# A one-core diffusion block: the residual's scale inside the gated additions, its gated bias in the next MLP quarter

## Chip, cores and metric

The kernel runs on one core of a Trainium2 chip. The metric is the device time of one execution in microseconds; the kernel before is given by the median of three runs. The profile is of one further execution of the same program.

## What is computed

The reference is one step of a one-layer backbone for 640 tokens (128 of a context, 512 of a latent) of width 1024: a token mixer, then a squared-ReLU MLP, each with a residual and a layer norm. The change touches only the residual of the MLP:

```python
h2 = layer_norm(x) * (1.0 + mod[:, 4]) + mod[:, 3]
f = jnp.square(jax.nn.relu(h2 @ w_mlp1 + b_mlp1)) @ w_mlp2 + b_mlp2
x = layer_norm(DEEPNORM_ALPHA * x + mod[:, 5] * f, ln2_g, ln2_b)
```

With gate g = mod[:, 5], the sum in the last line is alpha * x + g * b_mlp2 + g * (hidden @ w_mlp2). The gate differs between context and latent tokens, so there are two rows of it.

## The kernel before, in words

**Tiles and stages.** The 640 tokens lie in five tiles of 128 tokens; `x1s` holds them as five fp32 tiles of 128 x 1024. fp32 products are made in TensorE's fp32r format from two parts: `wsplit` (L324 to L329) has SP load a weight tile of 128 x 1024 (`wr`, two buffers), ACT casts its high part (L321) and DVE subtracts to get the low part (L322); both parts go to one tile (`wh`, three buffers). Three matmuls (high by high, high by low, low by high: `PASS`) make one product, and only the last of them needs DVE's low part.

**The MLP.** The hidden width of 4096 is done in four quarters of 1024. A quarter first makes its hidden tiles `fx` (eight of 128 rows, two parts each), then multiplies them by its quarter of `w_mlp2` (L1061 to L1076): for either half `fh` of the 1024 output columns there are four weight tiles (index `kp`), each with two steps of k, five token tiles and three passes, so 30 matmuls of 512 columns a weight tile, 120 a half and 240 a quarter (L1073). Below, a weight tile of the first half is called kp0 to kp3 and one of the second half kp0' to kp3'. A half's sums lie in PSUM: two tiles of two banks (`ps`, token tiles 0 and 1, then 2 and 3) and one bank. There are three of the two-bank tiles, so the second tile of the second half takes the place of the first tile of the first half, and may be written only after that one has been read by `add_gated` (L849 to L852): DVE multiplies the sum in PSUM by the gate (L851), then adds it to the `x1s` tile (L852).

**The first quarter** makes its hidden tiles with plain matmuls (L913, L926), and does three things besides. `gates` (L773 to L787) builds the two gate tiles `g5`: DVE adds a bias row (L778), the row goes to DRAM (`grd`, L779), and two DMAs spread it over the 128 partitions (L783). `rhs_sums` (L946 to L974), a generator that advances one step after each `wsplit`, makes sums of `h2` for the later quarters, whose first products use a scheme with fewer multiplications (`mlp_pair`, L999); its DVE lines are L953 to L972 and, through `split`, L322. And `residual` (L1042 to L1046) runs once, after the second weight tile: for each token tile DVE makes tmp = b2 * g5 (L1045) and x = alpha * x + tmp (L1046). Its row b2 is loaded at L1056 by `brow_tile` (L764 to L767), which repeats one row of DRAM over the 128 partitions. The second and third quarters take their hidden tiles from `mlp_in8`; the fourth is written apart and not touched.

**What sets the order.** Engines run their instructions in program order, one queue each. That order is not the text's: a scheduler, which works with the priorities of the text and a model of durations, places each instruction when the kernel is built, and tiles wait for a free buffer of their pool. The MLP's fp32 work tiles come from one pool of nine (`x4`); five are the `x1s` tiles, b2 and the tmp tiles are others.

Of the kernel before, what the change touches and what calls it, by code (L numbers as in the profile page):

```python
# [14 lines left out]
ALU = mybir.AluOpType  # L15
AX = mybir.AxisListType

P = 128
D = 1024
# [9 lines left out]
ALPHA = 2.0 ** 0.25  # L29
# [9 lines left out]
def hybrid_kernel(ctx: ExitStack, tc: tile.TileContext, xin, cc, w_ada0, w_ada, w_in, w_glu, w_pa, w_pool, w_pb,  # L39
                  w_out, w_m1, w_m2, cols, rows, brow, lam, bpk, cpk, ddg, s0, cst, invc, out, nstate):  # L40
    nc = tc.nc
    V, S, T = nc.vector, nc.scalar, nc.tensor
# [24 lines left out]
    def sub_tile(tag, bufs, pool=None):  # L67
        return lambda shape, name: (pool or sub[0]).tile(shape, F32, tag=tag, bufs=bufs, name=nm(name))
# [3 lines left out]
    def bank2(name="ps"):  # L72
        return pp[0].tile([P, 2, 512], F32, tag="mm", name=nm(name))
# [231 lines left out]
    for t in range(NTT):  # L305
        x = mat4([P, D], "x")
# [447 lines left out]
    x4 = sub_tile("x4", 9)  # L754
# [9 lines left out]
    def brow_tile(src, tile_of, name="brow"):  # L764
        t = tile_of([P, D], name)
        dma(t, src.broadcast_to([P, D]))
        return t  # L767
# [37 lines left out]
    for m in range(KT):  # L805
        ps = gps[m] if m < 2 else mm(wsplit(w_glu[m]), vx)
# [16 lines left out]
    x1s = []  # L823
    for t in range(NTT):
        x = x4([P, D], "x1")
# [3 lines left out]
    for m in range(KT):  # L829
# [4 lines left out]
        ps = mm(wsplit(w_pa[m]), [gx[:, k] for k in range(KT)])  # L834
# [7 lines left out]
        if m < NTT:  # L842
            tmp = x4([P, D], "tmp")
# [2 lines left out]
    ada4.cols(row_tile(), 3, True)  # L846


    def add_gated(x, g, ps, c0, c1):  # L849

        V.tensor_tensor(ps, ps, g[:, c0:c1], op=ALU.mult)  # L851
        V.tensor_tensor(x[:, c0:c1], x[:, c0:c1], ps, op=ALU.add)  # L852

    def ln_mv():
        return keep.tile([P, 2], F32, tag="mv", bufs=4, name=nm("mv"))
# [23 lines left out]
    for t in range(NTT):  # L879
        st = 0 if t else 1  # L880
        x = x1s[t]
        ps = bank2()
# [12 lines left out]
        tmp = x4([P, D], "tmp")  # L895
        V.tensor_scalar(tmp, x, mv[:, 0:1], rs, op0=ALU.subtract, op1=ALU.mult)
        hf = x4([P, KT, P], "h2f")
        for h in range(2):
            pt = bank("pst")
# [3 lines left out]
            for i in range(4):  # L903
                k = 4 * h + i
                S.activation(hf[:, k, :], pt[:, i * P:(i + 1) * P], AF.Identity,
                             scale=modc[:, 3, k, st:st + 1], bias=modc[:, 2, k, st:st + 1])
# [39 lines left out]
    def rhs_sums():  # L946
        b11, b12, b21, b22 = [h2[:, :, 4 * i:4 * i + 4, j * HN:(j + 1) * HN] for i in range(2) for j in range(2)]
        t1, t2, t4 = [w10("t").rearrange("p a (k c) -> p a k c", k=4) for _ in range(3)]
        rq.update(b11=b11, b21=b21, b22=b22, t1=t1, t2=t2, t3=b12, t4=t4)

        def whole(b, k):
            f = x4([P, 2, HN], "bf")
            V.tensor_tensor(f, b[:, 0, k:k + 2].bitcast(F32), b[:, 1, k:k + 2].bitcast(F32), op=ALU.add)  # L953
            return f

        def put(t, k, f):
            split(f, t[:, 0, k:k + 2], t[:, 1, k:k + 2])

        for k in (0, 2):
            f12, f11 = whole(b12, k), whole(b11, k)  # L960
            V.tensor_tensor(f11, f12, f11, op=ALU.subtract)
            put(t1, k, f11)
            yield
            f22 = whole(b22, k)
            V.tensor_tensor(f12, f22, f12, op=ALU.subtract)
            put(b12, k, f12)
            yield
            V.tensor_tensor(f22, f22, f11, op=ALU.subtract)
            put(t2, k, f22)
            yield  # L970
            f21 = whole(b21, k)
            V.tensor_tensor(f21, f21, f22, op=ALU.subtract)  # L972
            put(t4, k, f21)
            yield  # L974
# [64 lines left out]
    def mlp_in8(m):  # L1039
        return [f for i in range(0, 8, 2) for f in mlp_pair(m + i)]  # L1040

    def residual():  # L1042
        for t in range(NTT):
            tmp = x4([P, D], "tmp")
            V.tensor_tensor(tmp, b2, g5[0 if t else 1], op=ALU.mult)  # L1045
            V.scalar_tensor_tensor(x1s[t], x1s[t], ALPHA, tmp, op0=ALU.mult, op1=ALU.add)  # L1046

    for qf in range(3):
        if qf == 0:
            ada5.load(2)  # L1050
            fx = mlp_first()
            for i, n in ((5, 3), (6, 3), (7, 2)):
                ada5.step(n)
                if i == 7:
                    g5 = gates(ada5, 1)
                    b2 = brow_tile(brow[3:4, :], x4)  # L1056
                fx.append(mlp_in(i))
        else:
            fx = mlp_in8(qf * 8)
        sums = rhs_sums() if qf == 0 else iter(())  # L1060
        for fh in range(2):  # L1061
            pa, pb, pc_ = bank2(), bank2(), bank("ps4")
            pt = [pa[:, 0], pa[:, 1], pb[:, 0], pb[:, 1], pc_]
            for kp in range(4):
                hl = wsplit(w_m2[fh, qf * 4 + kp])
                next(sums, None)
                if qf + fh == 0 and kp == 1:
                    residual()
                for kk in range(2):
                    k = 2 * kp + kk  # L1070
                    for t in range(NTT):
                        for i, (wh, xh) in enumerate(PASS):
                            T.matmul(pt[t], fx[k][:, xh, t * P:(t + 1) * P], hl[:, wh, kk * 512:(kk + 1) * 512],  # L1073
                                     start=(k == 0 and i == 0), stop=(k == 7 and i == 2))
            for t in range(NTT):
                add_gated(x1s[t], g5[0 if t else 1], pt[t], fh * 512, fh * 512 + 512)  # L1076

    fx = mlp_in8(24)
    lg2, lb2 = brow_tile(brow[4:5, :], x4), brow_tile(brow[5:6, :], x4)
# [1 line left out]
    for t in range(NTT):  # L1081
        last = t == NTT - 1
        if t == 0:
            ps2 = bank2()
            ps = [ps2[:, 0], ps2[:, 1]]
        else:
            ps = [bank("pse")] + ([bank2()[:, 0], bank2()[:, 0]] if last else [bank("pse")])

        parts = [(0, 0, 512), (1, 0, 256), (1, 256, 256)] if last else [(0, 0, 512), (1, 0, 512)]
        x = x1s[t]  # L1090
        for k, n in [(k, n) for k in range(8) for n in range(2)] if t == 0 else \
                [(k, n) for n in range(len(parts)) for k in range(8)]:
            fh, o, ln = parts[n]
# [102 lines left out]
```

## Time and profile before

| | us |
|---|---|
| median of three runs | 1059.72 |
| the three runs | 1059.72, 1054.45, 1062.24 |
| the profiled execution | 1057.73 |
| its span | 1056.0 |
| first quarter's 240 output matmuls, first start to the next block's | 672.10 to 733.71 |

The span is the time between the first and the last instruction of the profiled execution; its own time has 1.7 us around it. Times within the trace count from the span's start. A row of the timeline merges instructions of one line: start, length, engine, line, operation, what it writes and reads, count, and in brackets the idle time of the engine before it with what ended that.

### The profile page before, as it was taken

The numbers are of one execution on the slowest core, as the hardware profiler recorded it, in microseconds if no ns is written. First come the engines' busy times: TensorE is split into PE (matmuls) and PEld (weight loads), VectorE is DVE, ScalarE is ACT, GpSimd is POOL, SyncE is SP. The second block draws the span as 40 slices with busy tenths as digits, with TensorE's granted clock in tenths as the row PEclk, the third lists the DMA queues.
The fourth block names the chain that finished last, engine by engine and source line by source line (L and its number), as shares of the span: only waits on it lengthen the run. The fifth ranks groups of instructions, "written<-read, shape, count | busy, mean of one in ns | idle before, by whom it ended". The sixth has DMA issues, their size and how long they took to land.

```text
span 1056.0 us, 18416 instructions
## 1 busy us (share of the span) xinstructions
PE 991.3 (94%) x7464; PEld 894.4 (85%) x7464; DVE 691.6 (65%) x1203; ACT 403.0 (38%) x683; POOL 110.9 (11%) x164
## 2 busy tenths in 40 slices
PE   4998989998998899999999999989999999999997
PEld 2887878988897799998987898868998899889886
DVE  7698769998921334545847955498864586458686
ACT  5457454322212534422222544313661266116610
POOL 0243210310069000300000000000000000000000
PEclk9999899999999798999999999999999999999999
DMA  9566666855498587977752134513222222212421
GB/s 362 191 176 179 168 182 194 255 166 170 119 284 248 161 253 244 360 231 252 247 182 83 31 110 155 150 45 100 81 100 73 68 80 100 80 60 81 162 78 60
DMA packets 117373, 166.85 MB, mean 158 GB/s; under 512 B 48104, under 2 KB 80872, under 8 KB 117288
## 3 DMA queue, kind: packets, MB, share of 16 engines
q1 hardware_dynamic: 111912, 146.27, 43.9%
q0 software_dynamic: 5376, 19.40, 5.4%
q8 instruction: 59, 0.97, 0.4%
q14 instruction: 26, 0.21, 0.1%
HBM read 135.30 MB, written 30.34 MB: 157 GB/s over the span
## 4 chain that ended last, share of the span: by engine, by line
PE 61%; DVE 16%; DMA 10%; issue 6%; ACT 5%; SPq 2%; DVEq 0%; ACTq 0%; POOL 0%; POOLq 0%
PE ps L336 20%; PE ps L1073 13%; PE ps L1006 8%; PE psx L1006 6%; PE pse L1096 3%; PE ps L886 3%; DVE wh L322 2%; DMA cf<-in_cpk_dram 2%; DMA yd<-y 2%; DVE ta L501 1%; DVE zt L504 1%; PE psa L236 1%; PE psz L480 1%; DVE ta L503 1%; PE ps L1096 1%
## 5 line engine op out<-in xcount | busy, mean ns | idle before, releaser
L336 PE MATMUL ps<-hk,wh 128*128 128x320 f32 x1344 | 217.1, 318 | 10.0 <-DVE sq L542 5.1
L336 PEld LDWEIGHTS ps<-hk,wh 128*128 128x128 f32 x1344 | 202.0, 192 | 18.6 <-issue 6.0
L322 DVE TENSOR_TENSOR wh<-wr,wh 128x1024 fp32r<-128x1024 f32 (+1 forms) x113 | 128.5, 1138 | 101.8 <-ACT wh L321 100.7
L321 ACT CAST wh<-wr 128x1024 fp32r<-128x1024 f32 (+1 forms) x113 | 109.3, 967 | 164.7 <-PE ps L1073 87.6
L1073 PE MATMUL ps<-wh,fx 128*128 128x512 f32 x720 | 166.1, 392 | 5.2 <-DVE x L852 3.0
L1073 PEld LDWEIGHTS ps<-wh,fx 128*128 128x128 f32 x720 | 135.7, 189 | 34.2 <-DVE x L852 3.4
L336 PEld LDWEIGHTS ps<-gx,wh 128*128 128x128 f32 x384 | 56.4, 187 | 3.3 <-issue 2.9
L336 PE MATMUL ps<-gx,wh 128*128 128x320 f32 x384 | 58.7, 310 | 0.0
L336 PEld LDWEIGHTS ps<-vx,wh 128*128 128x128 f32 x384 | 56.4, 188 | 2.5 <-ACT sg L813 2.1
L336 PE MATMUL ps<-vx,wh 128*128 128x320 f32 x384 | 58.1, 311 | 0.0
L224 POOL DMA_DIRECT2D wa<-in_w_ada_dram x32 | 16.9, 534 | 300.8 <-PE psa L236 110.2
L1006 PE MATMUL psx<-h,wh 128*128 128x320 f32 x288 | 47.5, 308 | 0.0
L1006 PE MATMUL ps<-h,w 128*128 128x320 f32 x288 | 46.5, 307 | 0.0
L438 POOL TENSOR_TENSOR cf<-cf 128x64 f32<-128x64 f32 x32 | 24.8, 776 | 191.0 <-DMA cf<-in_cpk_dram 95.7
L1006 PEld LDWEIGHTS psx<-h,wh 128*128 128x128 f32 x288 | 43.7, 187 | 0.2
L1006 PEld LDWEIGHTS ps<-h,w 128*128 128x128 f32 x288 | 43.2, 187 | 0.0
L573 PE MATMUL psy<-zt,q 64*128 64x80 f32 x512 | 42.1, 276 | 0.6 <-issue 0.6
L851 DVE TENSOR_TENSOR ps<-ps,gate 128x512 f32<-128x512 f32 (+2 forms) x39 | 28.1, 749 | 19.2 <-PE ps L1073 14.2
L573 PEld LDWEIGHTS psy<-zt,q 64*128 64x128 f32 x512 | 35.3, 190 | 4.2 <-issue 4.2
L886 PE MATMUL ps<-wo,mx 128*128 128x512 f32 x150 | 36.6, 392 | 0.7 <-ACT wo L321 0.7
L336 PE MATMUL ps<-ybx,wh 128*128 128x320 f32 x192 | 32.6, 328 | 2.7 <-ACT wh L321 2.7
L886 PEld LDWEIGHTS ps<-wo,mx 128*128 128x128 f32 x150 | 27.9, 188 | 7.2 <-ACT wo L321 1.5
(263 smaller groups left out, 1656.9 us busy)
## 6 DMA issues: line engine op xcount, KB each, us to landing
wr<-in_w_m_dram SPq DMA_DIRECT2D x64, 512.0 KB
wa<-in_w_ada_dram POOLq DMA_DIRECT2D x32, 512.0 KB, 5.0
wr<-in_w_in_dram SPq DMA_DIRECT2D x28, 512.0 KB
qd<-q SPq DMA_DIRECT2D x16, 512.0 KB
q<-qd SPq DMA_DIRECT2D x16, 512.0 KB
x<-in_xin_dram SPq DMA_DIRECT2D x10, 512.0 KB
wa<-in_w_ada_dram SPq DMA_DIRECT2D x10, 512.0 KB
tm<-sd SPq DMA_DIRECT2D x8, 512.0 KB
```

Source lines behind the costliest of these rows:

```text
L224: nc.gpsimd.dma_start(w, w_ada[self.mod, :, k * D:(k + 1) * D])
L236: T.matmul(self.ps[32 * q:32 * q + 32, 0:256], sc[:, k, :], w[:, q * 256:(q + 1) * 256], start=(k == 0), stop=(k == KT - 1), skip_group_ch ...
L321: S.copy(hi, raw)
L322: V.tensor_tensor(lo, raw, hi.bitcast(F32), op=ALU.subtract)
L336: T.matmul(ps[:, n, 0:ln], hl[:, wh, k * P:(k + 1) * P], xk[:, xh, o:o + ln], start=(k == 0 and i == 0), stop=(k == nk - 1 and i == 2))
L438: E.tensor_tensor(c[:, :, 3, :], c[:, :, 1, :], c[:, :, 2, :], op=ALU.add)
L573: T.matmul(o, q[d, l, i, :], zt[d, 0:NC // 2, i, 4 * e + l, :], start=(i == 0), stop=False, skip_group_check=True)
L851: V.tensor_tensor(ps, ps, g[:, c0:c1], op=ALU.mult)
L886: T.matmul(ps[:, n, :], mx[k][:, xh, t * P:(t + 1) * P], wo[k][:, wh, n * 512:(n + 1) * 512], start=(k == 0 and i == 0), stop=(k == KT - 1 ...
L1006: T.matmul(ps, hl[:, wh, c + k * P:c + (k + 1) * P], rq[b][:, xh, k, :], start=(start and k == 0 and i == 0), stop=(stop and k == 3 and i ...
L1073: T.matmul(pt[t], fx[k][:, xh, t * P:(t + 1) * P], hl[:, wh, kk * 512:(kk + 1) * 512], start=(k == 0 and i == 0), stop=(k == 7 and i == 2))
L1096: T.matmul(ps[n][:, 0:ln], fx[k][:, xh, t * P:(t + 1) * P], hl[:, wh, o_:o_ + ln], start=(k == 0 and i == 0), stop=(k == 7 and i == 2))
```

## The change

`residual` is gone. In the first quarter `add_gated` takes a scale: the second of its two instructions is then a scalar_tensor_tensor, x = alpha * x + ps, instead of an addition; since the columns are split between the two halves, each element of x is scaled once. The product of b2 and the gate is made once for either row of the gate (two tiles `bg`) instead of once for each token tile, and added to x by five plain additions in the second quarter, in a generator `biases` that advances one step after each weight tile of that quarter. The load of b2 moves into it.

```diff
-    def add_gated(x, g, ps, c0, c1):
+    def add_gated(x, g, ps, c0, c1, scale=None):
         V.tensor_tensor(ps, ps, g[:, c0:c1], op=ALU.mult)
-        V.tensor_tensor(x[:, c0:c1], x[:, c0:c1], ps, op=ALU.add)
+        if scale is None:
+            V.tensor_tensor(x[:, c0:c1], x[:, c0:c1], ps, op=ALU.add)
+        else:
+            V.scalar_tensor_tensor(x[:, c0:c1], x[:, c0:c1], scale, ps, op0=ALU.mult, op1=ALU.add)
...
-    def residual():
-        for t in range(NTT):
-            tmp = x4([P, D], "tmp")
-            V.tensor_tensor(tmp, b2, g5[0 if t else 1], op=ALU.mult)
-            V.scalar_tensor_tensor(x1s[t], x1s[t], ALPHA, tmp, op0=ALU.mult, op1=ALU.add)
+    def biases():
+        b2 = brow_tile(brow[3:4, :], x4)
+        bg = []
+        for st in range(2):
+            t = x4([P, D], "bg")
+            V.tensor_tensor(t, b2, g5[st], op=ALU.mult)
+            bg.append(t)
+            yield
+        for t in range(NTT):
+            V.tensor_tensor(x1s[t], x1s[t], bg[0 if t else 1], op=ALU.add)
+            yield
...
                     g5 = gates(ada5, 1)
-                    b2 = brow_tile(brow[3:4, :], x4)
...
-        sums = rhs_sums() if qf == 0 else iter(())
+        sums = rhs_sums() if qf == 0 else biases() if qf == 1 else iter(())
...
-                if qf + fh == 0 and kp == 1:
-                    residual()
...
-                add_gated(x1s[t], g5[0 if t else 1], pt[t], fh * 512, fh * 512 + 512)
+                add_gated(x1s[t], g5[0 if t else 1], pt[t], fh * 512, fh * 512 + 512, ALPHA if qf == 0 else None)
```

The scheduler then places DVE's instructions of the first quarter anew. First place: DVE before, from the residual to the first half's gated additions of the first quarter; `wh_7435` is the low part of kp0', `bf`, `t` and `h` are `rhs_sums`, `ps_7240` is the first half's sum of token tiles 0 and 1.

```order
L1045 TENSOR_TENSOR tmp_7310<-brow_7177,gate_7173 128x1024
L322 TENSOR_TENSOR t_7249<-bf_7293,t_7249 128x640
L1046 SCALAR_TENSOR_TENSOR x_781_5606<-x_781_5606,tmp_7310 128x1024
L953 TENSOR_TENSOR bf_7386<-h_6177 128x640
L322 TENSOR_TENSOR wh_7435<-wr_7434,wh_7435 128x1024
L972 TENSOR_TENSOR bf_7386<-bf_7386,bf_7293 128x640
L953 TENSOR_TENSOR bf_7439<-h_6177 128x640
L851 TENSOR_TENSOR ps_7240<-ps_7240,gate_7175 128x512
L322 TENSOR_TENSOR t_7250<-bf_7386,t_7250 128x640
L852 TENSOR_TENSOR x_777_5598<-x_777_5598,ps_7240 128x512
L851 TENSOR_TENSOR ps_7241<-ps_7241,gate_7173 128x512
L851 TENSOR_TENSOR ps_7240<-ps_7240,gate_7173 128x512
```
And DVE after the change, at the same place; `wh_7418` is kp0', `wh_7460` is kp1', `ps_7238` is the first half's sum of token tiles 0 and 1.

```order
L322 TENSOR_TENSOR wh_7418<-wr_7417,wh_7418 128x1024
L964 TENSOR_TENSOR bf_7424<-bf_7422,bf_7424 128x640
L956 TENSOR_TENSOR bf_7542<-h_6177 128x640
L968 TENSOR_TENSOR bf_7422<-bf_7464,bf_7422 128x640
L322 TENSOR_TENSOR t_7246<-bf_7424,t_7246 128x640
L971 TENSOR_TENSOR bf_7464<-bf_7464,bf_7424 128x640
L322 TENSOR_TENSOR h_6177<-bf_7422,h_6177 128x2x320
L975 TENSOR_TENSOR bf_7542<-bf_7542,bf_7464 128x640
L322 TENSOR_TENSOR t_7247<-bf_7464,t_7247 128x640
L322 TENSOR_TENSOR wh_7460<-wr_7459,wh_7460 128x1024
L322 TENSOR_TENSOR t_7248<-bf_7542,t_7248 128x640
L851 TENSOR_TENSOR ps_7238<-ps_7238,gate_7175 128x512
```
Before, the residual stands ahead of kp0's low part of the second half, and four instructions of `rhs_sums` stand between its fifth product and the first gated addition, a fifth behind that. After, kp0' stands further up, and between it and the gated additions there are nine instructions of `rhs_sums` and the low part of kp1', which was behind the additions before. Further up (not shown) the low part of kp2, in whose `wr` buffer kp0' is loaded, has moved behind four more instructions of 640 columns.

Second place: PE at the border of the two halves in the first quarter, before; `ps_7241` and `ps_972_7242` are the first half, `ps_7431`, `ps_995_7433` and `ps_7432` the second, and `ps_7432` takes the banks of `ps_7240`.

```order
L1073 MATMUL ps_7241<-wh_7382,fx_7237 128x512 x6
L1073 MATMUL ps_972_7242<-wh_7382,fx_7237 128x512 x3
L1073 MATMUL ps_7431<-wh_7435,fx_6970 128x512 x6
L1073 MATMUL ps_995_7433<-wh_7435,fx_6970 128x512 x3
L1073 MATMUL ps_7431<-wh_7435,fx_6977 128x512 x4
L1073 MATMUL ps_7432<-wh_7435,fx_6970 128x512 x6
```
The same place after; `ps_7415` takes the banks of `ps_7238`.

```order
L1080 MATMUL ps_7239<-wh_7365,fx_7235 128x512 x6
L1080 MATMUL ps_971_7240<-wh_7365,fx_7235 128x512 x3
L1080 MATMUL ps_7414<-wh_7418,fx_6970 128x512 x6
L1080 MATMUL ps_989_7416<-wh_7418,fx_6970 128x512 x3
L1080 MATMUL ps_7414<-wh_7418,fx_6977 128x512
L1080 MATMUL ps_7415<-wh_7418,fx_6970 128x512 x6
```
In the second half, PE reached the tile that waits for the gated additions after 13 matmuls; it reaches it after 10 with the change.

Third place: DVE in the second quarter, after the change, from the last hidden tile to the first half's gated additions; `fr_7997` is a hidden tile in the making, `fx` a finished one, `wh_8179`, `wh_8215`, `wh_8264` and `wh_8300` are kp2, kp3, kp0' and kp1'.

```order
L1029 TENSOR_TENSOR fr_7996<-ps_7995,fr_7997 128x320
L1051 TENSOR_TENSOR bg_8109<-brow_8107,gate_7173 128x1024
L1055 TENSOR_TENSOR x_778_5600<-x_778_5600,bg_8109 128x1024
L1032 TENSOR_TENSOR fr_7997<-ps_7995,fr_7997 128x320
L322 TENSOR_TENSOR fx_8092<-fr_7996,fx_8092 128x640
L322 TENSOR_TENSOR wh_8179<-wr_8178,wh_8179 128x1024
L1051 TENSOR_TENSOR bg_8146<-brow_8107,gate_7175 128x1024
L322 TENSOR_TENSOR fx_8096<-fr_7997,fx_8096 128x640
L1055 TENSOR_TENSOR x_777_5598<-x_777_5598,bg_8146 128x1024
L322 TENSOR_TENSOR wh_8215<-wr_8214,wh_8215 128x1024
L322 TENSOR_TENSOR wh_8264<-wr_8263,wh_8264 128x1024
L322 TENSOR_TENSOR wh_8300<-wr_8299,wh_8300 128x1024
```
Four of the new instructions stand here, the first two between the additions L1029 and L1032 of the last hidden pair (L1026 and L1029 before), which stood next to each other; the last three stand behind the first half's gated additions, around the low part of kp2'. On SP the load of b2 stands between the loads of kp2 and kp3 of this quarter.

## Rows read from the trace of the kernel before

**Rows 1.** The page's first part: busy time of each engine over the whole span.
```profile
PE 991.3 (94%) x7464; PEld 894.4 (85%) x7464; DVE 691.6 (65%) x1203; ACT 403.0 (38%) x683; POOL 110.9 (11%) x164
```

**Rows 2.** Chain that ended last, 660 to 745 us: start, length, what.
```profile
672.95 9.22 DMA gate<-grd
682.16 5.89 issue
...
690.42 2.27 DVE x L1046 x2
...
700.24 0.73 DVE bf L953
700.97 1.14 DVE wh L322
```

**Rows 3.** Timeline of PE, 672 to 736 us: start, length, line, count, [idle before].
```profile
672.10 27.82 PE L1073 MATMUL ps<-wh,fx 128*128 128x512 f32 x122
...
702.16 2.79 PE L1073 MATMUL ps<-wh,fx 128*128 128x512 f32 x11 [2.25 <-DVE wh L322]
...
707.96 25.91 PE L1073 MATMUL ps<-wh,fx 128*128 128x512 f32 x107 [3.00 <-DVE x L852]
...
733.71 1.92 PE L1006 MATMUL psx<-h,wh 128*128 128x320 f32 x12
```

**Rows 4.** Timeline of DVE and ACT, 688 to 691 us.
```profile
688.06 2.36 DVE L1045 TENSOR_TENSOR tmp<-brow,gate 128x1024 f32<-128x1024 f32 x2 [5.91 <-issue]
689.31 1.06 ACT L321 CAST wh<-wr 128x1024 fp32r<-128x1024 f32 x1 [7.89 <-DMA wr<-in_w_m_dram]
```

**Rows 5.** Timeline of SP's issues, 660 to 700 us.
```profile
672.53 0.93 SPq L783 DMA_DIRECT2D gate<-grd  x2
676.00 5.79 SPq L327 DMA_DIRECT2D wr<-in_w_m_dram  x2
```

**Rows 6.** Granted clock (column after PE busy) in chosen stretches, PE alone.
```profile
279.00:282.00 3.00, 0.83 (x6) 1.00 0.00 0
282.00:286.00 4.00, 3.92 (x27) 1.00 0.56 142
157.90:160.60 2.70, 0.10 (x2) 1.00 0.00 0
160.60:164.60 4.00, 4.00 (x42) 0.59 0.10 16
...
708.00:711.00 3.00, 3.00 (x7) 0.52 0.00 0
```

**Rows 7.** Instructions on tile tmp: ns min/median/max, first and last start.
```profile
L1045 DVE TENSOR_TENSOR tmp<-brow,gate x5: 1218/1219/1224, 688.1 to 697.1; 128x1024 f32<-128x1024 f32 x5
L1046 DVE SCALAR_TENSOR_TENSOR x<-x,tmp x5: 1217/1219/1219, 690.3 to 699.0; 128x1024 f32<-128x1024 f32 x5
```

**Rows 8.** Timeline of SP's issues, 775 to 785 us.
```profile
776.84 6.22 SPq L327 DMA_DIRECT2D wr<-in_w_m_dram  x2
```

**Rows 9.** Timeline of PE and DVE in the second quarter, 780 to 832 us.
```profile
782.62 0.48 DVE L1026 TENSOR_TENSOR fr<-ps,fr 128x320 f32<-128x320 f32 x1
...
785.02 47.36 PE L1073 MATMUL ps<-wh,fx 128*128 128x512 f32 x208
...
785.22 0.49 DVE L1029 TENSOR_TENSOR fr<-ps,fr 128x320 f32<-128x320 f32 x1 [2.11 <-PE ps L1006]
...
786.36 1.22 DVE L322 TENSOR_TENSOR wh<-wr,wh 128x1024 fp32r<-128x1024 f32 x1
...
808.82 0.70 DVE L851 TENSOR_TENSOR ps<-ps,gate 128x512 f32<-128x512 f32 x1 [2.45 <-PE ps L1073]
...
811.38 1.28 DVE L852 TENSOR_TENSOR x<-x,ps 128x512 f32<-128x512 f32 x2
...
814.96 1.22 DVE L322 TENSOR_TENSOR wh<-wr,wh 128x1024 fp32r<-128x1024 f32 x1
```

## Prediction

> **What bounds the kernel now.** I read the page first: PE is busy for 991.3 of 1056.0 us and DVE for 691.6 [rows 1], so DVE's own time counts only where PE stands idle for it. The change lies in the first two MLP quarters, so the next view is PE's timeline there [rows 3]. The first quarter's 240 output matmuls start at 672.10, and the next block starts at 733.71: 61.61 us. The second quarter gives the pace without a wait, 208 matmuls in 47.36 us, 0.2277 us each [rows 9]; 240 of them would take 54.65 us. So 6.96 us are lost in this quarter: 2.25 us idle until kp0' has its low part, 3.00 us idle until the first half's sums have been read by the gated additions, then 107 matmuls in 25.75 us (707.96 to 733.71) where the pace gives 24.36, thus 1.39 us, and some 0.3 us in the eleven between the waits [rows 3]. The 1.39 us are the clock: after the two waits TensorE had a mean of 0.52 over 708 to 711 us, which is its lower level of 1.2 GHz for nearly all of that time [rows 6].
>
> Why DVE is late there the chain tells [rows 2]: it runs from the second gate DMA over DVE's wait for it into the residual (one pair of its instructions at 690.42), then over what had queued behind it, a sum of `rhs_sums` at 700.24 and kp0' at 700.97. DVE stood 5.91 us idle before the first product of the residual and began it at 688.06 [rows 4]. The residual is five products and five scaled additions of 1.22 us each [rows 7], 12.2 us in all, and kp0' stands behind it in DVE's queue although its raw tile had landed at 689.31, where ACT began its cast [rows 4].
>
> **The change part by part.** *The residual goes.* In its stead the first reader of the gates is the first gated addition, whose sums cannot be there before 111 of the first half's 120 matmuls, at 672.10 + 111 x 0.2277 = 697.4; the gates were there by 688.06 [rows 4], so their landing has over 9 us of cover. What is late next is DVE's own list. The order after the change puts kp0' first, then nine 640-column instructions of `rhs_sums` and kp1', then the gated additions. All work out from the landing of the raw tile of kp0'. It was issued at 676.00 and used at 689.31, behind the two gate transfers issued at 672.53 [rows 4, 5]. Its buffer is freed by the low part of kp2, which now stands behind four more instructions of 640 columns; at a step of 0.73 us each [rows 2] that is 2.9 us later. Lateness of the landing: between 0 (the gates alone set it, and the b2 load no longer stands ahead of them) and 2.9 us. I take 0.5, near the lower end, because it was used 13.3 us after its issue but only 1.25 us after the gates had landed (688.06 to 689.31) [rows 4, 5], and they stand ahead of it as before. The cast then starts at 689.8, lasts 1.06 [rows 4], and kp0' costs a step of 1.14 [rows 2]: 692.0. Nine times 0.73 and 1.14 for kp1' are 7.7, with a little for those that read the instruction just before them 7.9: the gated additions start at 699.9. Six of them stand up to the one that frees the banks; in the second quarter these six went from 808.82 to 811.38 + 1.28 = 812.66, 3.84 us [rows 9]. So the banks are free at 703.8. PE gets to the matmul that needs them after 120 + 10, at 672.10 + 130 x 0.2277 = 701.7. The wait is 2.1 us, in place of 2.25, 3.00 and 1.7 us. At best it is 0, since additions that start at 697.4 would end at 701.2; at worst, with the whole 2.9 us, it is 4.5.
>
> *The clock.* After one idle stretch of 2.2 us (PE busy 0.83 of the 3.00 us to 282) the granted clock stayed at 1.00; after one of 2.6 us (busy 0.10 of 2.70) it was 0.59 over the next 4 us [rows 6]. A wait of 2.1 us stands nearer to the first, so I count nothing; the price if it falls is this stage's own 1.39 us.
>
> *The scale.* Ten additions become scalar_tensor_tensor. On 1024 columns this operation took 1219 ns in the residual and the product beside it 1219 ns [rows 7]; I take no difference. No row shows it with one operand in PSUM. Between nothing and one more addition each (two additions of 512 columns took 1.28 us [rows 9], so 0.64) three of them before the banks are freed give 0 to 1.9 us more wait.
>
> A rule of the Trainium skill speaks to this. The rows show scalar_tensor_tensor with two fp32 tiles of SBUF at the same 1219 ns as the product [rows 7]. The Vector Engine (DVE) Microarchitecture Reference, section "Points that are easy to get wrong", says that this instruction with two SBUF sources that are not bf16 halves its throughput. By the rows the sum stays; were the rule to hold here and for the PSUM operand too, the wait would be 4.0 us and the gain 3.0. The trace disagrees already for the SBUF case, so I leave it out.
>
> *The bias.* The second quarter gets two products and five additions of 1.22 us, 8.5 us on DVE. The first product and addition stand between L1026, which ended at 783.10, and L1029, before which DVE was idle for 2.11 us until 785.22 [rows 9]: they overrun by about 0.3 us. Behind them waits kp2, which was started at 786.36 and is needed at the 61st matmul, 785.02 + 53 x 0.2277 = 797.1 [rows 9]: over 9 us of cover. The next two lie in idle time before 808.82. The last three follow the gated additions; kp2' started at 814.96 and would be ready 2 x 1.14 later, at 818.5; it is needed at 785.02 + 173 x 0.2277 = 824.4 [rows 9]. Cost nothing. The load of b2 is issued behind that of kp2, which went at 776.84 [rows 8]. Its flight is not shown; the bounds are nothing and 13.3 us, the longest of a weight tile here (676.00 to 689.31 [rows 4, 5]). Even that lands at 790.5, and kp2 is ready at about 795.4, before 797.1. I take nothing, for both ends cost nothing. SP's next load behind it needs no new wait.
>
> The sum: 6.96 less 2.1 is 4.9 us off the profiled execution's 1057.73, 1052.8; scaled to the median of 1059.72, 1054.8.
>
> **Rivals.** *All of it goes*: DVE reaches the additions by 697.9 and PE never waits: 1059.72 - 7.0 = 1052.7. For it: 12.2 us leave a DVE that was late by 5. Against it: DVE had already been waiting for the transfers until 688 and 689, and the work behind is 7.9 us of sums.
>
> *Nothing goes*: the sums that were behind the additions now stand before them, and with kp0' 2.9 us later and the clock falling the losses are 4.5 + 1.39 = 5.9 of 6.96: 1058.6, no change. For it: the gate transfers still fill the queue.
>
> *Slower*: the raw tile of kp0' lands so late that DVE, which waits for it in order, keeps sums, kp1' and additions behind it. Each us of lateness is a us of PE's wait beyond 1.6. With the clock's 1.39 the loss equals 6.96 at 4.0 us, a landing at 693.3. At 6 us it is 9.0, so 1061.7. Against it: the issue moves by no more than 2.9 us.
>
> **How the numbers follow.** Forecast (a wait of 1 to 3.5 us in the first quarter, with or without the clock) 0.57; all of it 0.18; nothing 0.17; slower 0.08. The range: 1052.7 and 1061.7 are the ends of the cases; three runs of the kernel before lie between 1054.45 and 1062.24, so a median may fall 2 us off. I give 1050.5 to 1061. A measurement of this kernel tells about 1% (10.6 us) from no change. The whole loss in this quarter is 0.7%, so faster by over 1% asks for all of it and a favourable scatter: 0.06. Slower by over 1% asks for a landing some 14 us late: 0.02. Within 1%: 0.92.
>
> **What would show it.** Right: in the first quarter no PE wait for a low part, one wait of about 2 us ten matmuls into the second half, granted clock 1.00 behind it, and some 57 us from the first output matmul to the next block; in the second quarter an unbroken run of matmuls, with DVE's first product of b2 not waiting long. Wrong: a PE wait in the second quarter for kp2 or kp2', a scalar_tensor_tensor of 512 columns far above the 0.70 us of L851, or a cast of kp0' after 691.

## The result and the profile after

The kernel after took 1050.76 us in the median of 13 runs (1046.03 to 1056.02), the kernel before 1057.23 in 13 runs beside them: a ratio of 0.9945 (of the means of the two sets of runs), interval 0.9921 to 0.9968. That is 5.8 us faster, and the interval allows 3.4 to 8.4. The forecast gain was 4.9 us of 1059.72 (0.46%), the case "all of it goes" 7.0 us. The interval holds both, so the times don't tell these two apart; the traces do.

The page's first part of the kernel after, to be held against [rows 1]: PE is busy 2.7 us less, DVE 2.3 us less.

```profile
PE 988.6 (94%) x7464; PEld 893.0 (85%) x7464; DVE 689.3 (66%) x1200; ACT 403.1 (38%) x683; POOL 111.0 (11%) x164
```

The timeline of PE after, from the first output matmul of the first quarter to that of the next block, and in the second quarter (L1080 was L1073; the columns are those of [rows 3]):

```profile
673.71 54.60 PE L1080 MATMUL ps<-wh,fx 128*128 128x512 f32 x240
728.15 1.92 PE L1009 MATMUL psx<-h,wh 128*128 128x320 f32 x12
...
779.47 53.04 PE L1080 MATMUL ps<-wh,fx 128*128 128x512 f32 x233
```

One row with all 240 matmuls and no bracket stands where [rows 3] had three rows and two waits. From 673.71 to 728.15 are 54.44 us in place of 61.61: 7.17 us gained, a little over the 6.96 that the pace promised. Behind the quarter nothing moved: from the next block to the end of the span there were 1056.0 - 733.71 = 322.3 us before and 1050.3 - 728.15 = 322.2 after. The whole gain is in the first quarter. (The profiled execution gained only 1057.73 - 1052.09 = 5.64 us, since its first quarter began at 673.71, 1.61 us later than before. The kernels e4 and e5 below, whose edits come only after this quarter, began it at 676.46 and 677.01, so this is scatter between executions.)

DVE and ACT after, around kp0', to be held against [rows 4] and the chain [rows 2]:

```profile
688.24 1.05 ACT L321 CAST wh<-wr 128x1024 fp32r<-128x1024 f32 x1 [1.40 <-DMA wr<-in_w_m_dram]
689.32 1.23 DVE L322 TENSOR_TENSOR wh<-wr,wh 128x1024 fp32r<-128x1024 f32 x1 [1.04 <-ACT wh L321]
...
696.35 1.22 DVE L322 TENSOR_TENSOR wh<-wr,wh 128x1024 fp32r<-128x1024 f32 x1
697.48 0.82 DVE L322 TENSOR_TENSOR t<-bf,t 128x640 fp32r<-128x640 f32 x1
699.08 0.70 DVE L851 TENSOR_TENSOR ps<-ps,gate 128x512 f32<-128x512 f32 x1 [0.78 <-PE ps L1080]
...
701.65 1.28 DVE L855 SCALAR_TENSOR_TENSOR x<-x,ps 128x512 f32<-128x512 f32 x2
```

The bracket of L851 is the reading that matters. DVE waits for PE there, not PE for DVE: it had finished its list at 698.30 (697.48 + 0.82) and stood idle for 0.78 us. The sixth instruction that frees the banks ends at 701.65 + 1.28 = 702.93; PE needs them at 673.71 + 130 x 0.2277 = 703.31. The banks came free 0.4 us ahead, so the wait of 2.1 us that was forecast did not come. The granted clock from 704 us on (third column from the right), and SP's issue of kp0' (the first of four in the row):

```profile
704.00:728.00 24.00, 24.00 (x108) 19.88 (x107) 12.02 (x16) 4.72 (x5) 0.00 (x0) 1.00 0.26 88
```
```profile
680.59 17.33 SPq L327 DMA_DIRECT2D wr<-in_w_m_dram  x4
```

The clock is 1.00, against 0.52 in [rows 6]; ahead of 704 the row of 240 leaves no room for a fall. And kp0' shows what the forecast missed. Counted from the first output matmul it was issued at 680.59 - 673.71 = 6.88 us and its cast began at 14.53; in the kernel before it was issued at 3.90 and cast at 17.21 [rows 4, 5]. Issued 3.0 us later, it was there 2.7 us sooner. One trace of each would not be enough for this, but kernels with the same loads in the same order agree: with the order of before the cast came at 17.21, 17.23 (e7b below) and 17.32 (e3), with that of after at 14.53, 14.51 (e5) and 14.72 (e4).

The scaled addition and a plain one of the same shape, by tile (ns min/median/max):

```profile
L855 DVE SCALAR_TENSOR_TENSOR x<-x,ps x10: 676/680/689, 699.8 to 731.9; 128x512 f32<-128x512 f32 x10
L853 DVE TENSOR_TENSOR x<-x,pse x7: 673/686/689, 1005.7 to 1037.8; 128x512 f32<-128x512 f32 x7
```

Either form of the second instruction of `add_gated` takes the same time on 512 columns.

### The profile page after: what moved, and what is told of

Its sections match the earlier page's. It is cut to its first block, busy times and chain, and to the rows that moved or that the text cites. A ratio compares the mean times of both kernels' runs of the same rounds, so it can differ in the third digit from the quotient of the medians.

```text
span 1050.3 us, 18407 instructions
## 1 busy us (share of the span) xinstructions
PE 988.6 (94%) x7464; PEld 893.0 (85%) x7464; DVE 689.3 (66%) x1200; ACT 403.1 (38%) x683; POOL 111.0 (11%) x164
## 4 chain that ended last, share of the span: by engine, by line
PE 65%; DVE 12%; DMA 12%; issue 5%; ACT 4%; SPq 1%; POOL 0%; DVEq 0%; ACTq 0%; POOLq 0%
PE ps L336 19%; PE ps L1080 16%; PE ps L1009 8%; PE psx L1009 6%; PE ps L889 4%; PE pse L1103 3%; DMA wa<-in_w_ada_dram 3%; DMA cf<-in_cpk_dram 3%; DVE wh L322 2%; PE psy L573 2%; DVE ta L501 1%; DVE zt L504 1%; PE psz L480 1%; PE psa L236 1%; DVE ta L503 1%
## 5 line engine op out<-in xcount | busy, mean ns | idle before, releaser
L1080 PE MATMUL ps<-wh,fx 128*128 128x512 f32 x720 | 164.2, 390 | 0.0
L1080 PEld LDWEIGHTS ps<-wh,fx 128*128 128x128 f32 x720 | 135.0, 188 | 27.8
L851 DVE TENSOR_TENSOR ps<-ps,gate 128x512 f32<-128x512 f32 (+2 forms) x39 | 28.1, 749 | 20.7 <-PE ps L1080 15.8
L336 PEld LDWEIGHTS ps<-ybx,wh 128*128 128x128 f32 x192 | 30.8, 204 | 4.5 <-ACT wh L321 3.8
```

The lines of the kernel that those rows point to most:

```text
L336: T.matmul(ps[:, n, 0:ln], hl[:, wh, k * P:(k + 1) * P], xk[:, xh, o:o + ln], start=(k == 0 and i == 0), stop=(k == nk - 1 and i == 2))
```

## The experiments

Each was timed beside the kernel before, and its ratio is to those runs. Times "rel" count from the first output matmul of the first quarter in the same trace, since that start scatters.

**e7b_bias_in_place: the scale as in the change, the bias left where the residual stood.** The two products and five additions run at once behind the second weight tile of the first quarter, b2 loaded at its old place.

```diff
-        sums = rhs_sums() if qf == 0 else biases() if qf == 1 else iter(())
+        sums = rhs_sums() if qf == 0 else iter(())
...
+                if qf + fh == 0 and kp == 1:
+                    for _ in biases():
+                        pass
```

> The changed kernel with the bias left in the first quarter: the two products and five additions stand where the residual stood, and the load of b2 too; only the scale is in the gated additions. DVE has three products fewer than before, at the same place. My theory (what counts is what stands on DVE between the gates' landing and the gated additions): DVE begins the products when the gates land, some 16 us after the first output matmul, is through with seven instructions at 24, frees the banks only at about 36 against 29.6: a PE wait of 5 to 7 us and a dip of the clock, time 0.997 to 1.003 of the kernel before. Rival (the gain is that of fewer DVE instructions and of the fused scale): a good part of the gain stays, 0.995 to 0.997.

1058.47 us, ratio 0.9988 (0.9959 to 1.0018). DVE, then PE, then PE's granted clock behind the wait (the last three columns: clock, share of the DMA engines, GB/s):

```profile
686.91 1.23 DVE L1050 TENSOR_TENSOR bg<-brow,gate 128x1024 f32<-128x1024 f32 x1 [4.80 <-DMA gate<-grd]
688.06 5.76 DVE L1054 TENSOR_TENSOR x<-x,bg 128x1024 f32<-128x1024 f32 x5
...
701.89 1.29 DVE L851 TENSOR_TENSOR ps<-ps,gate 128x512 f32<-128x512 f32 x2
```
```profile
670.92 31.00 PE L1083 MATMUL ps<-wh,fx 128*128 128x512 f32 x136
706.21 26.30 PE L1083 MATMUL ps<-wh,fx 128*128 128x512 f32 x104 [4.29 <-DVE x L855]
```
```profile
706.30:709.00 2.70, 2.70 (x7) 0.50 0.00 0
```

Moving the scale and sharing the products, without moving the bias, is worth nothing that can be measured. The bias waits for the second gate in DVE's queue for 4.80 us, the additions begin at 30.97 rel (after: 25.37), and one wait of 4.29 us with a fallen clock takes the place of the two of before. That is the theory, though its wait was put at 5 to 7 us. The row also confirms a reading of the prediction: DVE began this product at 15.99 rel, and the trace names the gate as what it waited for; the first product of the kernel before began at 15.96, where [rows 4] name nothing.

**e3_share: the kernel before with its products shared.** Two products in place of five; the residual is seven instructions, 3.7 us less.

```diff
+        bg = []
+        for st in range(2):
+            tmp = x4([P, D], "tmp")
+            V.tensor_tensor(tmp, b2, g5[st], op=ALU.mult)
+            bg.append(tmp)
         for t in range(NTT):
-            tmp = x4([P, D], "tmp")
-            V.tensor_tensor(tmp, b2, g5[0 if t else 1], op=ALU.mult)
-            V.scalar_tensor_tensor(x1s[t], x1s[t], ALPHA, tmp, op0=ALU.mult, op1=ALU.add)
+            V.scalar_tensor_tensor(x1s[t], x1s[t], ALPHA, bg[0 if t else 1], op0=ALU.mult, op1=ALU.add)
```

> The kernel before with one edit: the residual makes the product of b2 and the gate twice instead of five times (seven instructions of 1024 columns in place of ten, 3.7 us less on DVE); scale, place and load stay. Theory A (DVE is late in the first quarter by what stands ahead of kp0' and of the additions): kp0' is ready 3.7 us sooner, so PE's first wait (2.25 us) goes; of the second wait some 1.5 to 3 us may stay or come back, since the order of the sums behind it changes with it: first quarter's output block 55 to 60 us (before 61.6), 0.995 to 0.999 of before. Theory B (only the move of the bias out of the quarter counts, a shorter residual is filled with other work by the scheduler): block 60 to 62 us, 0.998 to 1.001.

1058.04 us, ratio 0.9988 (0.9958 to 1.0017). PE, and DVE from kp0' on:

```profile
671.42 31.00 PE L1076 MATMUL ps<-wh,fx 128*128 128x512 f32 x136
706.80 26.10 PE L1076 MATMUL ps<-wh,fx 128*128 128x512 f32 x104 [4.38 <-DVE x L852]
732.74 1.92 PE L1006 MATMUL psx<-h,wh 128*128 128x320 f32 x12
```
```profile
695.80 1.21 DVE L322 TENSOR_TENSOR wh<-wr,wh 128x1024 fp32r<-128x1024 f32 x1
...
700.61 1.21 DVE L322 TENSOR_TENSOR wh<-wr,wh 128x1024 fp32r<-128x1024 f32 x1
...
702.48 1.28 DVE L851 TENSOR_TENSOR ps<-ps,gate 128x512 f32<-128x512 f32 x2
```

The block took 61.32 us, theory B by its number, though half of A was right. DVE began the low part of kp0' 4.4 us sooner (24.38 rel, before 28.79 in the same view) and PE's first wait went. But the scheduler put kp1' and more sums into the room ahead of the additions, which begin at 31.06 rel. The second wait grew from 3.00 to 4.38 us, and the clock fell behind it as before (0.50 over 706.9 to 709.0). A shorter residual only changes what is late.

**e4_no_bias and e5_at_once: what the bias costs in the second quarter.** e4 leaves out the term g * b_mlp2 altogether; e5 runs all seven instructions at that quarter's first weight tile.

```diff
 e4:
-        sums = rhs_sums() if qf == 0 else biases() if qf == 1 else iter(())
+        sums = rhs_sums() if qf == 0 else iter(())
 e5:
                 next(sums, None)
+                if qf == 1:
+                    for _ in sums:
+                        pass
```

> The changed kernel without the gated bias: the term g * b_mlp2 is left out, with its load, two products and five additions. My theory (in the second quarter this work lies wholly in DVE's idle time): as the changed kernel, 0.9945 of the kernel before, within 0.2%, PE's run of output matmuls in the second quarter as long as with the bias. Rival (8.5 us of DVE work delay something): faster than the changed kernel by 1 us or more, 0.993 or less, with a shorter second quarter.

> The changed kernel with the whole bias placed at the second quarter's first weight tile instead of one token tile after each weight tile. Theory (cover is large): DVE puts three more additions ahead of kp2, which is ready at about 12.7 us after the quarter's first output matmul and needed at 15.5: no PE wait, 0.9945. Rival (the spreading a token tile at a time is what keeps PE fed): a PE wait for kp2 or kp3 of 1 to 4 us, 0.996 or more.

e4 took 1052.84 us, ratio 0.9945 (0.9918 to 0.9973); e5 1052.68, 0.9940 (0.9915 to 0.9965). The second quarter's rows of PE, of e4 and of e5:

```profile
782.20 53.02 PE L1080 MATMUL ps<-wh,fx 128*128 128x512 f32 x233
```
```profile
782.78 53.04 PE L1083 MATMUL ps<-wh,fx 128*128 128x512 f32 x233
```

233 matmuls take 53.04 us with the bias a tile at a time, 53.02 without it, 53.04 with all of it at once. The bias is free there, and spreading it was not needed. e4 is within 0.2% of the kernel after, as expected, and e5 shows no wait.

**e6_first_quarter: the bias in the second half of the first quarter**, two steps behind each of its weight tiles, b2 loaded there.

```diff
-        sums = rhs_sums() if qf == 0 else biases() if qf == 1 else iter(())
+        sums = rhs_sums() if qf == 0 else iter(())
...
+                if qf == 0 and fh == 1:
+                    if kp == 0:
+                        bias = biases()
+                    next(bias, None)
+                    next(bias, None)
```

> The kernel after with the two products and five additions of the bias in the second half of the first quarter, two steps behind each of its weight tiles, in place of the second quarter (b2 is loaded there too). Nothing is left out. Theory A (what cost the time was DVE work ahead of the first half's gated additions, not the quarter as such): the 8.5 us stand behind kp0' of the second half; as far as the scheduler lets some of it go ahead of the gated additions (one product and one addition, 2.4 us) PE waits 0 to 2 us at the second half's eleventh matmul; 0.9945 to 0.997 of before. Theory B (DVE in the first quarter is full, so the bias anywhere in it costs what it cost before): a wait of over 3 us and the clock at its lower level behind it, 0.998 to 1.000.

1052.78 us, ratio 0.9926 (0.9903 to 0.9950). PE, and DVE:

```profile
676.31 54.60 PE L1085 MATMUL ps<-wh,fx 128*128 128x512 f32 x240
```
```profile
694.22 1.22 DVE L1051 TENSOR_TENSOR bg<-brow,gate 128x1024 f32<-128x1024 f32 x1
...
701.68 0.70 DVE L851 TENSOR_TENSOR ps<-ps,gate 128x512 f32<-128x512 f32 x1 [2.41 <-PE ps L1085]
...
707.83 1.22 DVE L1055 TENSOR_TENSOR x<-x,bg 128x1024 f32<-128x1024 f32 x1
```

Theory A at its better end by the trace, and a little below its range by the time: PE never waits. One product went ahead of the additions and DVE still stood 2.41 us for PE; the other product and the five additions lie behind them. So the quarter was not what cost the time; it was the work that had to be done ahead of the first half's additions.

**e2_load_back, e11_early_issue, e12_early_and_load: why kp0' landed sooner.** e2 puts an unread load of b2 back at its old place in the kernel after. e11 begins the steps of `rhs_sums` later, so that kp2's low part frees the buffer for kp0' sooner. e12 does both, and with that has the order on SP of the kernel before.

```diff
 e2, e12:
                     g5 = gates(ada5, 1)
+                    brow_tile(brow[3:4, :], x4)
 e11, e12:
-                next(sums, None)
+                for _ in range({(0, 0): 0, (0, 1): 0, (0, 2): 1, (0, 3): 2}.get((fh, kp), 2) if qf == 0 else 1):
+                    next(sums, None)
```

> The changed kernel with one thing added: the load of b2 stands where it stood before the change (ahead of the gate transfers), into a tile that nobody reads; the order on DVE is that of the changed kernel. Times are counted from the first quarter's first output matmul. In the kernel before, ACT began the cast of kp0' 17.2 us after it, in the changed one 14.5. Theory A (the b2 load ahead of the gates held the gates and kp0' up): the cast moves back to about 17; DVE then reaches the six additions at about 17.2 + 1.06 + 1.14 + 7.9 = 27.3 and frees the banks at 31.1, against 29.6 where PE wants them: one PE wait of about 1.5 us, time 0.996 of the kernel before. Theory B (the cast is sooner because kp0' was issued later, when the gates were nearly through): the cast stays near 14.5, no PE wait, time 0.9945.

> The kernel after with the steps of rhs_sums begun later in the first quarter (none behind the first two weight tiles, one and two behind the next, then two each), so that kp2's low part stands earlier on DVE and frees the buffer for kp0' some 3 us earlier; the order on SP is the same, nothing is left out. kp0' should be issued about 3.5 us behind the first output matmul, as in the kernel before (3.9), where the kernel after issued it 6.9 us behind it. Theory A (a weight tile that is issued early, while the gate transfers have hardly begun, shares the queues with them and both land late, as before): its cast starts about 17 us behind the first output matmul (after: 14.5), the gated additions begin about 2 us later than in the kernel after, PE waits 0.5 to 2.5 us ten matmuls into the second half, and the time is 0.996 to 0.998 of before. Theory B (the landing in the kernel before was late for another reason, such as the load of b2 or the later gate row): the cast starts at 11 to 14.5 us, no wait of PE, 0.9945 of before.

> The early issue (e11) and the unread load of b2 at its old place (e2) together, in the kernel after: SP's order is then that of the kernel before, with kp0' issued about 3.4 to 3.9 us behind the first output matmul. Only the extra transfer is added, nothing left out. Alone, the early issue made the cast of kp0' start 15.7 us behind the first output matmul and the load 14.8, against 14.5 in the kernel after and 17.2 in the kernel before. Theory A (the two compound: a weight tile put on the queues while the gate transfers have only begun is slow, and the load of b2 ahead of them makes that worse): cast at 16.8 to 17.4, additions from about 27, a wait of PE of 0.8 to 1.5 us, 0.994 to 0.997 of before. Theory B (they only add up): cast at 15.8 to 16.2, wait under 0.4 us, and some 1.2 us of the kernel before's lateness come from something else, DVE's or ACT's place for instance.

e2: 1052.99 us, ratio 0.9949 (0.9927 to 0.9971). e11: 1053.05, 0.9927 (0.9902 to 0.9951). e12: 1052.35, 0.9939 (0.9915 to 0.9963). The timeline of e2, e11 and e12 in turn: PE's output matmuls, SP's issue of kp0' (the first of four in its row), its cast on ACT, and for e12 the first gated addition:

```profile
671.06 54.59 PE L1081 MATMUL ps<-wh,fx 128*128 128x512 f32 x240
...
677.94 17.64 SPq L327 DMA_DIRECT2D wr<-in_w_m_dram  x4
...
685.89 1.05 ACT L321 CAST wh<-wr 128x1024 fp32r<-128x1024 f32 x1 [1.71 <-DMA wr<-in_w_m_dram]
```
```profile
675.07 54.93 PE L1081 MATMUL ps<-wh,fx 128*128 128x512 f32 x240
...
678.43 22.17 SPq L327 DMA_DIRECT2D wr<-in_w_m_dram  x4
...
690.77 1.05 ACT L321 CAST wh<-wr 128x1024 fp32r<-128x1024 f32 x1 [3.00 <-DMA wr<-in_w_m_dram]
```
```profile
674.45 29.64 PE L1082 MATMUL ps<-wh,fx 128*128 128x512 f32 x130
...
677.82 23.65 SPq L327 DMA_DIRECT2D wr<-in_w_m_dram  x4
...
691.63 1.05 ACT L321 CAST wh<-wr 128x1024 fp32r<-128x1024 f32 x1 [4.47 <-DMA wr<-in_w_m_dram]
...
701.76 0.70 DVE L851 TENSOR_TENSOR ps<-ps,gate 128x512 f32<-128x512 f32 x1
...
705.62 25.23 PE L1082 MATMUL ps<-wh,fx 128*128 128x512 f32 x110 [1.54 <-DVE x L855]
730.70 1.92 PE L1009 MATMUL psx<-h,wh 128*128 128x320 f32 x12
```

With the load of b2 in front the cast began at 14.83 rel against 14.53, so theory B of e2; the 0.3 us are hardly more than the scatter, since kernels without that load ahead of the gates have 14.51 to 14.95 (e6). The early issue costs 1.2 us (15.70), between the two theories of e11: late, but not as late as before, and its block is only 0.3 us longer (54.93 against 54.60). Both together cost 2.65 us (17.18, where the kernel before had 17.21). They compound, theory A of e12 (its wait just above the range given), and that is the whole of the kernel before's lateness. Part of it is that the gates themselves set out later behind the load of b2: SP waited 2.1 us until their row was in DRAM, in e11 1.4, and issued them at 0.59 rel in e12, at -0.17 in e11.

With this landing the change has a wait of 1.54 us, and its block, from 674.45 to 730.70, takes 56.25 us in place of 61.61. By this pair of traces 5.4 of the 7.2 us gained come from the residual's leaving, and the other 1.8 from the sooner landing. The times do not resolve the difference.

**e9_late_tile, e13_later_tile: the rival on the other side, made to happen.** One copy of a part of a gate tile to unused DRAM stands between the gates and kp0' on SP, or five.

```diff
 e9:
                     g5 = gates(ada5, 1)
+                    dma(mbd[0], g5[1][:, 0:NT])
 e13:
+                    for m in range(5):
+                        dma(mbd[m], g5[1][:, 0:NT])
```

> The kernel after with one more DMA on SP, which copies a part of the gate tile (128x640) to DRAM that nothing reads, right behind the two gate transfers: SP waits for the gates to land before it issues kp0'. It makes the rival named slower of the prediction happen. Both theories: kp0' is issued about 15 to 16 us behind the first output matmul in place of 6.9. Theory A (all of DVE's list works out from the landing, each us of lateness is a us of wait of PE): its cast starts at 18.5 to 21, 4 to 6.5 us later than in the kernel after; the additions are late by the same, less the 0.8 us that DVE waited for PE; PE waits 3 to 6 us ten matmuls into the second half (or part of it at kp0' itself, needed at 27.3 us, if the landing is later still), with 1 to 1.5 us more for the clock at its lower level behind it: 0.998 to 1.001 of before. Theory B (the sums behind kp0' have slack, since the scheduler or the transfers let them go ahead): wait under 1.5 us, 0.995 to 0.996.

> As e9, but with five copies of a part of the gate tile (128x640 each) to DRAM that nothing reads, behind the gates and ahead of kp0': the raw tile is issued some 1.7 us later than in e9 and shares the queues with 1.3 MB more. Nothing is left out. In e9 the cast started at 16.33 us behind the first output matmul, DVE began the gated additions 9.98 us later (26.31), and PE waited 0.53. Theory A (each us of lateness beyond e9's is a us of wait of PE): cast at 19.5 to 22, a wait of PE of 3.5 to 6 us at the second half's eleventh matmul, the clock at its lower level for some us behind it (1 to 1.5 us more), the quarter's output block 59 to 62 us: 0.997 to 1.001 of before. Theory B (the rest of the sums can go ahead or the additions have slack): wait under 2.5 us, 0.994 to 0.996.

e9: 1051.08 us, ratio 0.9901 (0.9865 to 0.9936, from only four runs of it, and below what either theory expected). e13: 1058.32, 1.0000 (0.9977 to 1.0023). The same rows of the timeline of e9 and of e13, then PE's granted clock in e13 behind its wait:

```profile
672.12 29.64 PE L1081 MATMUL ps<-wh,fx 128*128 128x512 f32 x130
...
683.76 14.37 SPq L327 DMA_DIRECT2D wr<-in_w_m_dram  x4
...
688.45 1.05 ACT L321 CAST wh<-wr 128x1024 fp32r<-128x1024 f32 x1 [3.21 <-DMA wr<-in_w_m_dram]
...
698.43 0.69 DVE L851 TENSOR_TENSOR ps<-ps,gate 128x512 f32<-128x512 f32 x1
...
702.28 25.23 PE L1081 MATMUL ps<-wh,fx 128*128 128x512 f32 x110 [0.53 <-DVE x L855]
```
```profile
674.30 29.64 PE L1082 MATMUL ps<-wh,fx 128*128 128x512 f32 x130
...
688.47 14.77 SPq L327 DMA_DIRECT2D wr<-in_w_m_dram  x4
...
693.55 1.06 ACT L321 CAST wh<-wr 128x1024 fp32r<-128x1024 f32 x1 [6.11 <-DMA wr<-in_w_m_dram]
...
703.53 0.70 DVE L851 TENSOR_TENSOR ps<-ps,gate 128x512 f32<-128x512 f32 x1
...
707.40 26.84 PE L1082 MATMUL ps<-wh,fx 128*128 128x512 f32 x110 [3.46 <-DVE x L855]
...
734.07 1.92 PE L1009 MATMUL psx<-h,wh 128*128 128x320 f32 x12
```
```profile
707.40:709.50 2.10, 2.10 (x6) 0.58 0.00 0
```

e9 missed its numbers: the gates without company had landed by 11.2 rel (SP waits for them and then issues the copy, at 683.32), not at 15 to 16, and kp0' then flew only 4.7 us, so its cast was 1.8 us late, not 4 to 6.5. By the wait (0.53 us) that is theory B's number, but not for B's reason: theory A's step from the landing to the wait held. From the cast to the additions it is 9.98 us in e9, 9.98 in e13 and 10.13 in e12; e13's cast is 2.92 us later than e9's (19.25 rel against 16.33) and its wait 2.93 us longer. In e13 the clock also falls, and 110 matmuls take 26.67 us (to 734.07) in place of 25.05 (110 x 0.2277). e13 is theory A, its wait just under the 3.5 us put as the least. Its block of 59.77 us takes back 5.3 of the 7.17 us gained, and the time cannot be told from that of the kernel before.

## Why the prediction was right, and where not

*What bounds the kernel there: right.* The loss of 6.96 us in the first quarter was DVE's lateness and the clock behind it. All of it went, 7.17 us by the trace, and nothing moved behind the quarter. The forecast was that 4.9 would go. That the ratio measured (0.9945) lies so near to the forecast's (0.9954) is in part luck: the block's 7.17 us alone would make 0.9932, and the interval holds all three.

*The residual goes, and work out from the landing of kp0': right.* Where the landing was made late, the forecast's own steps came out: from the cast to the additions it put 10.1 us (689.8 to 699.9), measured 9.98 to 10.13; from there to the free banks 3.84, measured 3.80 in e12 (701.76 to 705.62, less the 0.06 by which PE starts behind them). e12, the change with the landing of before (17.2 rel, where the forecast put 17.7), has the one wait ten matmuls into the second half that the forecast drew, 1.54 us for 2.1, and a block of 56.25 us for "some 57".

*"Lateness of the landing: between 0 and 2.9 us, I take 0.5": the step that failed.* Measured: 14.53 rel against 17.21, so 2.7 us sooner. The whole bracket lay on one side: its lower end stood at 0, although no reason excluded a gain. Of the lead of 3.2 us over the 17.7 assumed, 2.1 remove the wait, and the rest is DVE's idle 0.78 and the 0.4 by which the banks are early. The argument was that the gates stand ahead and set the landing, and that issuing later can at best cost nothing. Its first half held more exactly than the rows before could show: in every run that issued kp0' before the gates were in, the cast began 1.67 to 1.73 us behind the gates' last packet (ten kernels; five of them in the table below). What failed is that the gates' own landing was left where it had been. The runs showed in its place that they landed 2.7 us sooner (12.84 rel against 15.53) when kp0' was issued with about half of their transfer done and no load of b2 ran ahead of them; the early issue alone gave 14.02, the load alone 13.16, both 15.45. That the issue of kp0' would move by 2.9 us was right (3.0).

*The clock: as forecast, but for want of a wait.* There was no fall in the kernel after. At 1.54 us of idle time (e12) the 110 matmuls kept their pace, at 3.46 (e13) the granted clock was 0.58 behind it, mostly the lower level of 1.2 GHz. The forecast's 2.1 us lies between and was not tried.

*The scale: right.* 680 ns with one operand in PSUM, the additions 686 ns; the forecast's upper bound of 1.9 us more wait is gone. The rule that the prediction weighed (the Trainium skill, Vector Engine (DVE) Microarchitecture Reference, "Points that are easy to get wrong") says half throughput for two SBUF sources that are not bf16. [Rows 7] show no such cost beside the product of the same shape on 1024 columns; with a source in PSUM, which the rule does not name, there is none beside the addition either.

*The bias: right.* Free in the second quarter (e4, e5), the load of b2 with it. SP issued that load at 771.67, and DVE's first product of b2 followed the hidden tile's addition with no wait, so the load took under 5.8 us where the bound was 13.3:

```profile
777.47 1.22 DVE L1051 TENSOR_TENSOR bg<-brow,gate 128x1024 f32<-128x1024 f32 x1
```

e6 adds that the bias would have been free in the first quarter too, behind the additions.

*The rivals.* "All of it goes" is what PE's timeline shows, and was given 0.18. It was argued down because DVE had been waiting for transfers until 688 and 689, with 7.9 us of sums behind; those waits were themselves partly of the kernel's own making, as the landings above show. Its own reason, that 12.2 us leave DVE, would not have been enough: e12 loses the same work and still waits. "Nothing goes" did not happen, but e13 shows its like: a landing at 19.25 rel takes back three quarters in the trace, and the rest is less than the time tells. "Slower" asks for a landing beyond 21.2 rel (693.3), which e13 did not reach; its slope, a us of wait for a us of lateness, is shown.

No version beat the kernel after by more than the scatter (e9's lower ratio, of four runs, has an interval that overlaps): in its first quarter no wait of PE is left to take away.

## What to carry to other kernels

Work that waits for a late transfer in an in-order queue is dear by what stands behind it, not by its own length: shortening the residual by 3.7 us or taking its scale out gave nothing, putting it behind the additions that free the banks gave 5.4 us, and the sooner landing that came with it the other 1.8. Where a change moves a load, bound its landing on both sides of zero: a later issue can land sooner when transfers ahead of it share the queues. And test a freed wait by asking who waits at the same spot afterwards: here the bracket turned from PE behind DVE into DVE behind PE.

## What the runs showed of the hardware that was not expected

The two loads that spread the gates over the partitions (512 KB each) and kp0' (512 KB) interfere, and more so the earlier kp0' joins them. All times are rel; the flight is from issue to cast, and in each row the cast's wait was for this transfer. The gates move in 1024 packets of 1 KB, so the last packet of that size in the trace's record of packets is theirs; e9's copy, which waits for them, was issued 0.33 us behind it.

| kernel | b2 load ahead | gates issued | kp0' issued | gates' last packet | cast | flight |
|---|---|---|---|---|---|---|
| before | yes | 0.43 | 3.90 | 15.53 | 17.21 | 13.3 |
| e12 | yes | 0.59 | 3.37 | 15.45 | 17.18 | 13.8 |
| e11 | no | -0.17 | 3.36 | 14.02 | 15.70 | 12.3 |
| e2 | yes | 0.37 | 6.88 | 13.16 | 14.83 | 8.0 |
| after | no | -0.16 | 6.88 | 12.84 | 14.53 | 7.7 |
| e9 | one copy | -0.16 | 11.64 | 10.87 | 16.33 | 4.7 |

In the first five rows the cast is 1.67 to 1.73 us behind the gates' last packet. So an earlier issue did not bring kp0' ahead of the gates; with the gates later, both were late.

What all queues moved in these flights, kp1' and the rest included, of the kernel before, of the one after and of e9 (stretch, length, clock, share of the DMA engines, GB/s):

```profile
676.00:689.30 13.30, 1.00 0.51 132
```
```profile
680.60:688.20 7.60, 1.00 0.82 185
```
```profile
683.80:688.50 4.70, 1.00 0.81 279
```

With a fifth of the gates' packets done at the issue of kp0' (before), the queues moved 132 GB/s at half their engines' time; with the gates landed, 279. The gates alone moved 94 GB/s in e9 (672.0 to 683.3), so the mixture is faster than they are by themselves, but less than half as fast as kp0', kp1' and the copy behind them. What in the queues makes the early mixture slow no run here tells; that it does, and that 6.9 us was better than 3.4 and than 11.6, the table shows.
